# State-space mixer of a streaming encoder: parameters of ten pairs issued ahead of the mixer's inputs, outputs by way of DRAM in large transfers, sines and decays made one stage ahead of their use

## The chip, the cores and the metric

One NeuronCore of one Trainium2 chip runs the whole program in one launch. The metric is device time in microseconds (us), the median of several executions. The kernel before takes 2367.25 us (three runs, 2365.27 to 2368.46). The profile is of one execution of its own.

## The reference

Two layers of an encoder work on 1024 prompt positions and 64 sample positions, 1088 columns in all, of width 1024. Layer 0 mixes by sliding-window attention, layer 1 by a state-space mixer (S5), and each layer ends in a gated convolutional FFN. The change lies in the mixer of layer 1 alone:

```python
xr = jnp.einsum('blgi,gpi->blgp', u_blk, bbr)
xi = jnp.einsum('blgi,gpi->blgp', u_blk, bbi)
...
_, _, sr, si = lax.associative_scan(_affine_combine, (ar, ai, xr, xi), axis=1)
y = jnp.einsum('blgp,gip->blgi', sr, cr) - jnp.einsum('blgp,gip->blgi', si, ci)
...
z = jax.nn.gelu(y).astype(h.dtype)
ag = z @ w_glu + b_glu
out = ag[..., :D_MODEL] * jax.nn.sigmoid(ag[..., D_MODEL:])
```

There are 64 groups of 16 channels, each with a complex state of 64 dimensions that runs along the positions. The final states are outputs too.

## The kernel before, in words

All activations lie with channels on the partitions. Matrix products are done in three passes on split operands (`mm3`, L181 to L183): a high part and a remainder of each operand in a rounded format. So each weight tile of 512 KB is loaded as `raw` (L169, L173), copied to its high part by ScalarE (L175), and its remainder is made by VectorE (L176). `whl` is the pair of both.

**The mixer's stage** (`ssm`) stands between two stretches of dense matmuls: the down projection of the first FFN, and the GLU product of the mixer (`pb`, `pa`). It works on 32 pairs of groups.

- Ahead of it, the normalised input is written to DRAM in a layout by blocks of 8 positions (`hd<-xs`, L873) and read back as four tiles `U` (L917), each of 16 groups, 137 columns (128 prompt blocks, a gap, 8 sample blocks). The row factor is multiplied in afterwards, 8 groups at a time (`ssm_scale`, L923). The factors (`sel`) are ready only when the norm of the last block of columns is.
- The parameters of each pair (522 KB) were worked out during the first FFN and lie in DRAM as `prm`. `params(t)` loads those of two pairs into one tile `pm` of the tag "big", by two DMAs (L952).
- A batch is two pairs (the first two and the last two pairs are batches of one; so there are 18 batches). It goes through stages, with a `yield` between them, and `staged` lets the batches follow each other by one stage. Stage one: ScalarE makes the sines `sc` with both signs (L966) and the decays `rd` (L969); TensorE makes `p1` (L985); VectorE multiplies by cosines (L986) and sines (L990) and adds (L991). Stage two: VectorE runs the scan (L1004) and turns back with two products (L1007, L1008); ScalarE picks the final states into `fin` (L1011). Stage three: TensorE makes `p3` from `U` (L1018, two matmuls a pair) and from the two products (L1023, sixteen a pair); ScalarE copies it into `ys` (L1027). On the page `p1` and `p3` are both called `p`.
- After each fourth pair (a group of 8 channel groups, numbered `kt`, 0 to 7), `ys` is brought into channel order: eight DMAs of 16 partitions each from SBUF to SBUF (`yf<-ys`, L1032). Two stages later ScalarE computes the GELU `z` (L1041, L1043) and its high part `zh` (L1048), and VectorE the remainder `zl` (L1049). These are the operands of the GLU product.

**What sets the order.** Each engine has one in-order queue; a scheduler fixes it when the program is built, from the order in the code and from `self.order(x, first)`, which only forbids x to stand ahead of `first` on an engine. All these loads and stores are issued by SP's queue (SyncE), in order: an entry that has to wait for a semaphore holds all behind it. The order list `turns` puts `sc` and `rd` of a batch behind `fin` of the batch before. The tag "big" has six buffers, shared by `whl`, `pm` and one `U` tile; a `pm` can be loaded once an earlier user of its buffer is done. `sc` and `rd` have two buffers each, PSUM tiles of `p3` six, `p1` two. `U` number 2 lies in "big", number 3 in the buffer of an FFN result (tag "ypB") that has first to be spilled to DRAM (`x<-y`, L1198).

## Time and profile before

| | |
|---|---|
| median of three runs | 2367.25 us (2365.27 to 2368.46) |
| the profiled execution: its own time | 2367.1 us |
| its span (first to last instruction) | 2365.3 us |
| TensorE busy | 2269.7 us, 96% |
| VectorE busy | 1463.6 us, 62% |
| ScalarE busy | 893.6 us, 38% |
| last matmul of the down projection ahead of the mixer | 1197.4 us |
| first matmul of the mixer's pairs | 1222.6 us |
| first matmul of the GLU product | 1354.9 us |

PE is TensorE, DVE is VectorE, ACT is ScalarE, SP is SyncE's queue. "Busy" counts the time in which an instruction of the engine ran. `[7.28 <-X]` behind a row of the timeline says that the engine stood idle for 7.28 us before it, and that X ended that. PEclk is the clock that TensorE was granted, as a share of full speed. A row of the grouped view gives: line, engine, operation, output and inputs, shapes, count; then busy us in total and mean ns of one; then idle us just before them, and what ended it.

### The profile page before, as it was taken

How to read it: one execution, taken by the hardware profiler on the slowest of the kernel's cores; microseconds unless marked ns; L12 is line 12 of the kernel's file. 1: busy time of each engine (PE TensorE's matmuls, PEld its weight loads, DVE VectorE, ACT ScalarE, POOL GpSimd, SP SyncE). 2: the span in 40 equal slices, each digit the busy share in tenths (PEclk: the TensorE clock that was granted, in tenths of full speed). 3: DMA queues.
4: the chain of work that ended last, by engine and by line, in shares of the span. 5: the costliest groups of instructions: out<-in, count | busy, mean ns of one | idle time of the engine just before them, and what ended most of it. 6: DMA issues, size and time to landing. Idle time of an engine off the chain costs nothing. (4 is left out here: it accounts for less than half of the span.)

```text
span 2365.3 us, 35852 instructions
## 1 busy us (share of the span) xinstructions
PE 2269.7 (96%) x14265; PEld 2201.1 (93%) x14265; DVE 1463.6 (62%) x2836; ACT 893.6 (38%) x1463; POOL 282.1 (12%) x286
## 2 busy tenths in 40 slices
PE   8999999999999999999957799999999999999997
PEld 7987799999999999999955699999999999999997
DVE  8677649897577776464557812586555555465554
ACT  5256635322333334444525621343222222154332
POOL 5222006000122311020000100240000000000000
PEclk9999999999999999999967899999999999999998
DMA  5000015322334345664567521242222221165652
GB/s 189 33 30 19 28 50 183 109 69 102 101 130 146 121 137 173 213 213 151 187 209 236 149 70 37 72 157 86 76 82 73 84 73 64 51 211 180 211 176 96
DMA packets 167702, 282.52 MB, mean 119 GB/s; under 512 B 22800, under 2 KB 105264, under 8 KB 167408
## 3 DMA queue, kind: packets, MB, share of 16 engines
q1 hardware_dynamic: 165504, 273.41, 35.9%
q0 software_dynamic: 2032, 6.83, 0.8%
q8 instruction: 112, 1.84, 0.3%
q14 instruction: 54, 0.44, 0.1%
HBM read 210.03 MB, written 65.68 MB: 117 GB/s over the span
## 5 line engine op out<-in xcount | busy, mean ns | idle before, releaser
L181 PE MATMUL mm<-hl,whl 128*128 128x384 f32 (+1 forms) x2232 | 734.9, 330 | 15.5 <-DVE hl L247 8.2
L183 PE MATMUL mm<-hh,whl 128*128 128x384 f32 (+1 forms) x2232 | 733.3, 329 | 1.9 <-DVE whl L176 1.9
L182 PE MATMUL mm<-hh,whl 128*128 128x384 f32 (+1 forms) x2232 | 735.0, 329 | 0.0
L175 ACT ACTIVATE whl<-raw 128x1024 fp32r<-128x1024 f32 x256 | 269.9, 1058 | 707.9 <-PE mm L183 587.9
L176 DVE TENSOR_TENSOR whl<-raw,whl 128x1024 fp32r<-128x1024 f32 x256 | 321.1, 1257 | 224.9 <-ACT whl L175 224.6
L181 PEld LDWEIGHTS mm<-hl,whl 128*128 128x128 f32 x2232 | 420.2, 188 | 17.7 <-DVE hl L247 10.3
L183 PEld LDWEIGHTS mm<-hh,whl 128*128 128x128 f32 x2232 | 420.1, 188 | 2.8 <-DVE whl L176 2.7
L182 PEld LDWEIGHTS mm<-hh,whl 128*128 128x128 f32 x2232 | 420.4, 188 | 0.4
L181 PE MATMUL mm<-gt,whl 128*128 128x384 f32 (+1 forms) x1056 | 346.3, 328 | 2.9 <-ACT y L392 2.3
L182 PE MATMUL mm<-gt,whl 128*128 128x384 f32 (+1 forms) x1056 | 345.5, 327 | 0.0
L183 PE MATMUL mm<-gt,whl 128*128 128x384 f32 (+1 forms) x1056 | 342.6, 327 | 0.7 <-DVE whl L176 0.7
L295 DVE TENSOR_TENSOR u<-rb,mm 128x384 f32<-128x384 f32 (+1 forms) x264 | 132.0, 507 | 285.6 <-PE mm L183 285.4
L181 PEld LDWEIGHTS mm<-gt,whl 128*128 128x128 f32 x1056 | 198.2, 188 | 4.3 <-ACT y L392 2.8
L183 PEld LDWEIGHTS mm<-gt,whl 128*128 128x128 f32 x1056 | 197.9, 188 | 1.0 <-DVE whl L176 1.0
L182 PEld LDWEIGHTS mm<-gt,whl 128*128 128x128 f32 x1056 | 198.3, 188 | 0.0
L303 ACT ACTIVATE t<-u,ppt 128x1090 f32<-128x1090 f32 x88 | 113.5, 1289 | 29.0 <-DVE u L297 15.7
L304 DVE SCALAR_TENSOR_TENSOR t<-u,ppt,t 128x1090 f32<-128x1090 f32 x88 | 119.0, 1352 | 8.6 <-ACT t L303 8.6
L305 DVE SCALAR_TENSOR_TENSOR t<-u,ppt,t 128x1090 f32<-128x1090 f32 x88 | 119.0, 1352 | 1.7
L266 POOL TENSOR_TENSOR y<-y,xl 128x768 f32<-128x768 f32 (+1 forms) x18 | 32.1, 1789 | 622.3 <-DVE y L264 321.7
L318 ACT ACTIVATE t<-t 128x1090 f32<-128x1090 f32 x44 | 49.0, 1114 | 101.0 <-DVE t L305 101.0
L1079 DVE SCALAR_TENSOR_TENSOR y<-pa,ppt,sg 128x384 f32<-128x384 f32 (+1 forms) x24 | 14.2, 594 | 99.6 <-ACT sg L1078 99.6
L1023 PE MATMUL p<-wk,pm 64*128 64x137 f32 x512 | 50.5, 351 | 23.3 <-DVE wk L1007 9.3
(315 smaller groups left out, 3299.0 us busy)
## 6 DMA issues: line engine op xcount, KB each, us to landing
raw<-in_w_down SPq DMA_DIRECT2D x132, 512.0 KB, 4.0
raw<-in_w_up SPq DMA_DIRECT2D x88, 512.0 KB, 3.3
gd<-t SPq DMA_DIRECT2D x44, 512.0 KB, 2.6
pm<-prm SPq DMA_DIRECT2D x32, 522.0 KB, 5.5
gr<-gd SPq DMA_DIRECT2D x28, 384.0 KB, 4.5
xl<-x SPq DMA_DIRECT2D x24, 384.0 KB, 4.0
raw<-in_w_glu SPq DMA_DIRECT2D x16, 512.0 KB, 4.3
gr<-gd SPq DMA_DIRECT2D x22, 320.0 KB, 4.4
```

The costliest lines, as they stand in the source:

```text
L175: nc.scalar.activation(w[:, 0], raw, AF.Copy)
L176: nc.vector.tensor_sub(w[:, 1], raw, w[:, 0].bitcast(F32))
L181: nc.tensor.matmul(out, w[:, 0, sl], xl, start=start, stop=False)
L182: nc.tensor.matmul(out, w[:, 0, sl], xh, start=False, stop=False)
L183: self.last_mm = nc.tensor.matmul(out, w[:, 1, sl], xh, start=False, stop=stop)
L266: by[q].tensor_add(y[:, 2 * q:2 * q + 2], y[:, 2 * q:2 * q + 2], xs[q])
L295: nc.vector.tensor_mul(u[:, t0 + 2:t0 + 2 + np_], rb[:, t0:t0 + np_], ps[:, :np_])
L303: nc.scalar.activation(t, u[:, 0:T + 2], AF.Identity, bias=cb(m), scale=cw(0, m))
L304: nc.vector.scalar_tensor_tensor(t, u[:, 1:T + 3], cw(1, m), t, op0=ALU.mult, op1=ALU.add)
L305: nc.vector.scalar_tensor_tensor(t, u[:, 2:T + 4], cw(2, m), t, op0=ALU.mult, op1=ALU.add)
L318: nc.scalar.activation(ta, ta, AF.Gelu_apprx_tanh)
L1023: nc.tensor.matmul(p3[e], pm[r, i, o:o + P], g_[r, i, c, 0:NC_], start=False, stop=c == 1 and s == 1)
```

## The change

Four things change, all in `ssm` and `ssm_load`.

1. `params` becomes `load`. The `pm` tiles of five steps (ten pairs) are issued at the top of the stage, ahead of the writes and reads of the inputs; then each step t issues tile t+5.
2. `fins[-2]` replaces `turns[0]`: `sc` and `rd` of a batch stand behind `fin` of the batch before the last.
3. `ys` goes to DRAM by one DMA of ScalarE's own queue (`yd<-ys`, L1035) and comes back as `yf` by one DMA of SP (`yf<-yd`, L1040), one stage later, behind a `pm` load. The GELU follows three stages behind instead of two, and behind the last `yd` write issued.
4. `U` number 2 and number 3 change places ("ypB" and "big"), the spill moves ahead of `U` 2, `U` 3 is loaded from step 6 on, and the first two weight tiles of the GLU stand behind the last `pm`.

```diff
-        if q == 2:
+        if q == 3:
             u = self.big([P, 16, NC_], "U", F32)
         else:
-            u = self.yp.tile([P, 16, NC_], F32, name="U", tag="ypB" if q == 3 else "ypA", bufs=1 if q == 3 else 2)
+            u = self.yp.tile([P, 16, NC_], F32, name="U", tag="ypB" if q == 2 else "ypA", bufs=1 if q == 2 else 2)
...
+        yd = self.dram.tile([D, 8, NC_], F32, name="yd")
...
+            tiles, got, fins, out = {}, {}, [self.last_rs] * 2, [None]
+
+            def load(t):
+
+                pm = self.big([P, 2, PRM], "pm", F32)
+                for e in range(2):
+                    got[t] = nc.sync.dma_start(pm[:, e], self.prm[:, 2 * t + e])
+                tiles[t] = [pm]
+            for t in range(5):
+                load(t)
+            self.order(self.hw[0], got[4])
             us = [self.ssm_load(0)]
...
                 if e0 == 0:
-                    params(t)
+                    if t + 5 < 16:
+                        load(t + 5)
...
                 for c in range(2):
                     x = nc.scalar.activation(sc[:, :, c], pm[:, :, OSI:PRM], AF.Copy, scale=(1.0, -1.0)[c])
-                    self.order(x, turns[0])
+                    self.order(x, fins[-2])
                 for e, q in enumerate(qs):
                     x = nc.scalar.activation(rd[:, e], mask[:, None, :].to_broadcast([P, 2, 138]), AF.Copy, scale=self.rho[:, q:q + 1])
-                    self.order(x, turns[0])
+                    self.order(x, fins[-2])
                 if qs[-1] == 31:
                     self.wsrc.pop(0)
-                    self.load_ahead(AHEAD)
+                    for j in range(AHEAD):
+                        self.load_ahead(1 + j)
+                        self.order(self.loaded, got[15])
...
                 if qs[0] == 2:
+                    self.order(self.spill(), self.last_u)
                     us.append(self.ssm_load(2))
-                if qs[0] == 4:
-                    self.order(self.spill(), self.last_u)
+                if qs[0] == 12:
                     us.append(self.ssm_load(3))
...
-                turns[0] = x
+                fins.append(x)
...
+                    out.append(nc.scalar.dma_start(yd[kt * P:kt * P + P].rearrange("(g i) t c -> (i t) g c", i=16), ys[0]))
                     yf = self.t4([P, 8, NC_], "yf")
-                    for g_ in range(8):
-                        x = nc.sync.dma_start(yf[16 * g_:16 * g_ + 16], ys[0][:, g_])
-                        if g_ == 0:
-                            yx.append((kt, x))
+
                     if kt < 7:
-
+                        yield
+                    x = nc.sync.dma_start(yf, yd[kt * P:kt * P + P])
+                    if t + 6 in got:
+                        self.order(x, got[t + 6])
+                    if kt < 7:
                         yield
                         yield
...
                     self.order(x, out[0])
+                    self.order(x, out[-1])
```

**SP's queue at the start of the mixer's stage**, as a difference (+ is the changed kernel, - the kernel before; `hd` and `U` are the inputs on their way through DRAM, `pm` the parameters):

```order
-L952 DMA pm<-prm 128x1044 x4
+L937 DMA pm<-prm 128x1044 x12
 L873 DMA hd<-xs 128x1096 x2
 L917 DMA U<-hd 128x8x137
+L873 DMA hd<-xs 128x2x1096 x2
+L917 DMA U<-hd 128x8x137
 L873 DMA hd<-xs 128x2x1096
-L917 DMA U<-hd 128x8x137
-L873 DMA hd<-xs 128x2x1096 x2
-L917 DMA U<-hd 128x8x137 x4
-L952 DMA pm<-prm 128x1044 x2
-L1198 DMA x_91<-y 1024x1x320
```

Twelve parameter loads (six tiles; the sixth is that of step 0's `load(5)`) instead of four stand ahead of the first write of the inputs, and the second half of `U` 0 stands behind two more writes.

**ScalarE's queue in the middle of the stage.** Before, `wk_11998` holds pairs 14 and 15, and `sc_12071` and `rd_12072` belong to pairs 16 and 17:

```order
L1011 COPY fin_11455<-wk_11998 128x8 x2
L966 ACTIVATE sc_12071<-pm_12068 128x2x138 x2
L969 ACTIVATE rd_12072<-mask_11456,rho_276 128x276 x2
L1027 ACTIVATE ys_12107<-p3_12095 128x137
L1027 ACTIVATE ys_12107<-p3_12096 128x137
L1027 ACTIVATE ys_12107<-p3_12110 128x137
L1027 ACTIVATE ys_12107<-p3_12111 128x137
L1041 ACTIVATE z_12157<-yf_12054 128x1024
```

In the changed kernel `wk_11925` holds pairs 12 and 13, `sc_12053` and `rd_12054` belong to pairs 16 and 17 again, and `z_12077` is the GELU of `kt` 2:

```order
L1016 COPY fin_11471<-wk_11925 128x8 x2
L969 ACTIVATE sc_12053<-pm_11710 128x2x138 x2
L972 ACTIVATE rd_12054<-mask_11472,rho_276 128x276 x2
L1032 ACTIVATE ys_11965<-p3_12015 128x137
L1032 ACTIVATE ys_11965<-p3_12016 128x137
L1016 COPY fin_11471<-wk_11996 128x8
L1032 ACTIVATE ys_11965<-p3_12029 128x137
L1032 ACTIVATE ys_11965<-p3_12030 128x137
L1035 DMA yd_11442<-ys_11965 128x8x137
L1016 COPY fin_11471<-wk_11996 128x8
L1048 ACTIVATE z_12077<-yf_11910 128x1024
```

The sines of pairs 16 and 17 stand one `fin` earlier, and a DMA issue stands among ScalarE's instructions, ahead of the GELU of the group before.

**VectorE's queue at the end of the stage**, from the last product of the last batch of two on. Before:

```order
L1008 TENSOR_TENSOR wk<-wk,sc 128x552
L990 TENSOR_TENSOR wk<-sc,p_12497 128x2x137
L991 TENSOR_TENSOR wk<-wk 128x2x137
L1004 SCALAR_TENSOR_TENSOR wk<-rd,wk 128x276
L1007 TENSOR_TENSOR wk<-wk,pm 128x276
L1008 TENSOR_TENSOR wk<-wk,sc 128x276
L990 TENSOR_TENSOR wk<-sc,p_12555 128x2x137
L991 TENSOR_TENSOR wk<-wk 128x2x137
L1004 SCALAR_TENSOR_TENSOR wk<-rd,wk 128x276
L1007 TENSOR_TENSOR wk<-wk,pm 128x276
L1008 TENSOR_TENSOR wk<-wk,sc 128x276
```

In the changed kernel:

```order
L1013 TENSOR_TENSOR wk<-wk,sc 128x552
L176 TENSOR_TENSOR whl<-raw,whl 128x1024
L996 TENSOR_TENSOR wk<-wk 128x2x137
L991 TENSOR_TENSOR wk<-pm,p_12514 128x2x137
L1058 TENSOR_TENSOR zl<-z,zh 128x384 x2
L1058 TENSOR_TENSOR zl<-z,zh 128x320
L1009 SCALAR_TENSOR_TENSOR wk<-rd,wk 128x276
L995 TENSOR_TENSOR wk<-sc,p_12514 128x2x137
L1012 TENSOR_TENSOR wk<-wk,pm 128x276
L996 TENSOR_TENSOR wk<-wk 128x2x137
L1013 TENSOR_TENSOR wk<-wk,sc 128x276
L1009 SCALAR_TENSOR_TENSOR wk<-rd,wk 128x276
```

The two single pairs run side by side, and remainders of weights and of `z` that stood elsewhere stand between their steps. Before the last product of the stage VectorE has made four weight remainders (L176) in the kernel before and five in the changed one; of the sets of `zl`, six in both. On TensorE's queue, nine matmuls of the GLU stand ahead of the last group of `p3` matmuls before; in the changed kernel 23 stand ahead of the last six of them.

More of the change, by code (lines that the diff above doesn't have):

```diff
@@ L945, in ssm @@
             ROWS = (slice(0, 64), slice(64, 128))
-            tiles, got, turns, out = {}, {}, [self.last_rs], [None]
-            def params(t):
-                pm = self.big([P, 2, PRM], "pm", F32)
-                for e in range(2):
-                    got[t] = nc.sync.dma_start(pm[:, e], self.prm[:, 2 * t + e])
-                sc = self.wts.tile([P, D], F32, name="sc", tag="raw", bufs=2) if t < 8 else self.yp.tile([P, D], F32, name="sc", tag="ypA", bufs=2)
-                sc = sc[:, :552].rearrange("p (e c k) -> p e c k", e=2, c=2)
-                rd = sp.tile([P, 2, 2, 138], F32, name="rd", bufs=2)
-                tiles[t] = pm, sc, rd
             def batch(qs):
@@ L961, in batch @@
                 if e0 == 0:
-                    params(t)
+                    if t + 5 < 16:
+                        load(t + 5)
+                    sc = self.wts.tile([P, D], F32, name="sc", tag="raw", bufs=2) if t < 8 else self.yp.tile([P, D], F32, name="sc", tag="ypA", bufs=2)
+                    tiles[t] += [sc[:, :552].rearrange("p (e c k) -> p e c k", e=2, c=2), sp.tile([P, 2, 2, 138], F32, name="rd", bufs=2)]
                 pm, sc, rd = tiles[t]
@@ L1042, in batch @@
                     self.order(x, out[0])
+                    self.order(x, out[-1])
                     x = nc.scalar.activation(z[:, SEQ:].rearrange("p (c t) -> p c t", t=8), yv[:, 129:137], AF.Gelu_apprx_tanh)
                     self.order(x, out[0])
+                    self.order(x, out[-1])
                     for b, (t0, n_) in enumerate(BLK):
@@ L1049, in batch @@
                         nc.vector.tensor_sub(zl[b][:, kt], z[:, t0:t0 + n_], zh[b][:, kt].bitcast(F32))
-            yx, scans = [], []
+            scans = []
             self.staged([batch(x) for x in [[0], [1]] + [[q, q + 1] for q in range(2, 30, 2)] + [[30], [31]]], oldest=True)
-            for kt, x in yx:
-                if kt < 5:
-                    self.order(x, got[2 * kt + 6])
             fo = sp.tile([P, P], F32, name="fo")
```

## The prediction

> **What bounds the kernel now.** The page comes first, for the span, and then the windows over the mixer's stage, fifty microseconds a row.
>
> ```profile
> span 2365.3 us, 35852 instructions
> 1200.00:1250.00 50.00, 27.14 (x188) 22.16 (x189) 32.00 (x63) 16.64 (x48) 5.08 (x16) 0.59 0.81 268
> 1250.00:1300.00 50.00, 33.41 (x310) 28.05 (x310) 34.02 (x57) 25.89 (x73) 2.15 (x12) 0.76 0.74 220
> 1300.00:1350.00 50.00, 35.20 (x376) 29.67 (x373) 42.92 (x69) 30.42 (x86) 6.46 (x15) 0.91 0.55 163
> 1350.00:1400.00 50.00, 50.00 (x317) 48.98 (x316) 15.52 (x26) 18.74 (x37) 0.55 (x1) 0.96 0.26 79
> ```
>
> The columns are the stretch, its length, busy PE, weight loads, DVE, ACT and POOL, then the granted clock, the DMA share and GB/s. From 1350 on TensorE is full, and the GLU product and the second FFN behind it are the same instructions in both kernels. So the time that the mixer's stage saves or loses ahead of its first GLU matmul moves the end of the kernel by as much. In the three rows before that no engine is full; VectorE is the busiest in the second and third. The grouped view of 1222 to 1355 us says what it does and what it waits for.
>
> ```profile
> L1023 PE MATMUL p<-wk,pm 64*128 64x137 f32 x496 | 49.3, 353 | 23.3 <-DVE wk L1007 9.3 <-DVE wk L1008 8.0 <-issue 3.3
> L1018 PE MATMUL p<-U,pm 128*128 128x137 f32 x128 | 25.7, 345 | 7.7 <-ACT ys L1027 7.7
> L985 PE MATMUL p<-U,pm 128*64 128x137 f32 x256 | 23.3, 324 | 6.8 <-DMA pm<-prm 2.4 <-issue 2.3 <-PE p L1023 0.9
> L1004 DVE TENSOR_TENSOR_SCAN wk<-rd,wk 128x552 f32<-128x552 f32 (+1 forms) x18 | 21.2, 1179 | 1.4
> L986 DVE TENSOR_TENSOR wk<-pm,p 128x274 f32<-128x274 f32 x32 | 13.2, 433 | 4.1 <-DMA hd<-xs 2.2 <-PE p L985 1.5 <-issue 0.5
> L990 DVE TENSOR_TENSOR wk<-sc,p 128x274 f32<-128x274 f32 x32 | 13.0, 436 | 11.8 <-ACT sc L966 11.8
> L991 DVE TENSOR_TENSOR wk<-wk 128x548 f32<-128x548 f32 (+1 forms) x18 | 12.0, 666 | 1.8
> L1007 DVE TENSOR_TENSOR wk<-wk,pm 128x552 f32<-128x552 f32 (+1 forms) x17 | 11.5, 679 | 0.3
> L1008 DVE TENSOR_TENSOR wk<-wk,sc 128x552 f32<-128x552 f32 (+1 forms) x17 | 11.5, 678 | 0.3
> L923 DVE TENSOR_TENSOR U<-U,sel 128x1096 f32<-128x1096 f32 (+2 forms) x9 | 10.3, 1155 | 1.7 <-ACT sel L907 1.7
> L1049 DVE TENSOR_TENSOR zl<-z,zh 128x384 fp32r<-128x384 f32 (+1 forms) x18 | 9.0, 529 | 12.3 <-ACT zh L1048 12.3
> L176 DVE TENSOR_TENSOR whl<-raw,whl 128x1024 fp32r<-128x1024 f32 x4 | 4.9, 1219 | 0.0
> ```
>
> VectorE's rows sum to 21.2 + 13.2 + 13.0 + 12.0 + 11.5 + 11.5 + 10.3 + 9.0 + 4.9 = 106.6 us of work in 133 us. The idle column sums to 33.7 us, more than the 26.4 left over, because neighbouring instructions overlap a little. Of that idle time 24.1 us stand in two rows, and both name ScalarE: 11.8 us for the sines, 12.3 us for `zh`. Yet ScalarE worked only 16.64 + 25.89 + 30.42 = 73 us of 150 in the windows: it is late, not busy. Its timeline shows why.
>
> ```profile
> 1264.59 1.28 ACT L1041 ACT_TABLE_LOAD   x1 [7.28 <-DMA pm<-prm]
> 1265.89 2.03 ACT L1041 ACTIVATE z<-yf 128x1024 f32<-128x1024 f32 x1
> 1268.45 0.89 ACT L1048 ACTIVATE zh<-z 128x384 fp32r<-128x384 f32 x2
> ...
> 1269.01 0.56 DVE L1049 TENSOR_TENSOR zl<-z,zh 128x384 fp32r<-128x384 f32 x1 [7.92 <-ACT zh L1048]
> 1281.23 0.79 DVE L990 TENSOR_TENSOR wk<-sc,p 128x274 f32<-128x274 f32 x2 [4.16 <-ACT sc L966]
> ...
> ACT z L1041 <- DMA yf<-ys: 6.2, 2, 3.4
> ```
>
> The first GELU stands at the head of ScalarE's queue and waits 7.3 us for a transfer. The releaser is given as `pm<-prm`, but `z` reads only `yf`, whose eight issues stand in SP's queue between `pm` loads (1032 between 952); behind it wait `ys`, `fin` and the sines, and VectorE loses 7.92 us before its first `zl`; the second GELU costs it 4.16 us at the sines in the same way. The other wait recurs in every batch; here is one, from VectorE's timeline and ScalarE's.
>
> ```profile
> 1301.96 0.73 DVE L1008 TENSOR_TENSOR wk<-wk,sc 128x552 f32<-128x552 f32 x1
> 1303.61 0.79 DVE L990 TENSOR_TENSOR wk<-sc,p 128x274 f32<-128x274 f32 x2 [0.93 <-ACT sc L966]
> 1302.72 0.20 ACT L1011 COPY fin<-wk 128x8 f32<-128x8 f32 x1 [1.14 <-DVE wk L1008]
> 1302.83 0.75 ACT L966 ACTIVATE sc<-pm 128x276 f32<-128x276 f32 x2
> ```
>
> VectorE ends L1008, ScalarE copies the final states, only then makes the next sines, and VectorE stands still for 0.93 us.
>
> **The sines and decays.** With `fins[-2]` the sines of a batch stand behind the `fin` of a batch that VectorE left a whole batch ago, about 82.4 us (the first six VectorE groups) over 16 batches' worth of pairs = 5.15 us earlier. Two buffers each suffice: the one that is needed was last read by the batch before the last. So the 0.93 us wait goes, and with it nearly all of the 11.8 us; I leave 1 us for the first batches. **Gain 10.8 us** (bounds 7, if the 4.16 us that the second GELU causes there come back, and 11.8).
>
> **The outputs through DRAM.** Eight issues become one write by ScalarE and one read by SP, and the GELU moves back by one batch. These rows bound the trip (KB each, median us from issue to landing).
>
> ```profile
> pm<-prm SPq DMA_DIRECT2D x32, 522.0 KB, 5.5
> U<-hd SPq DMA_DIRECT2D x8, 548.0 KB, 8.6
> yf<-ys SPq DMA_DIRECT2D x64, 68.5 KB, 3.2
> hd<-xs SPq DMA_DIRECT2D x2, 548.0 KB, 3.2
> ```
>
> The write has the size of a `hd` write (3.2 us), the read that of a `pm` load (5.5): 8.7 us, or 17.2 if both were like the `U` reads, which ran while the DMA was full. From `kt` 3 on the read is ordered behind a `pm` load that needs `p3` of the next batch, so one batch more: 106.6 / 16 = 6.7 us + 5.5 = 12.2. The GELU stands behind the next group's `yd`, two batches or 13.3 us later. So it is covered by 1 to 4 us, and the 7.92 of the 12.3 us that VectorE lost at the first GELU goes; the other 4.4 us, in three places, are `zl` standing close behind `zh`, and I leave them. **Gain 7.9 us** (bounds: nothing, to 12.3).
>
> On ScalarE the write's issue is new. An issue on SP took this long:
>
> ```profile
> L917 SPq DMA_DIRECT2D U<-hd x8: 359/924/4535, 1214.0 to 1245.8; - x8
> ```
>
> That is 0.36 to 4.5 us, median 0.9. Eight times 0.9 us are 7 us more on an engine that idles half the time; with the read's thin cover I put **1.5 us lost** for both (bounds 0 and 16; the upper end is the second rival).
>
> The Trainium skill, "Perfetto Trace Analysis", section "DMA Instruction — HWDGE", says that the issuing sequencer is held from the moment its semaphores are met, first for the lock of a descriptor generator used by one issuer at a time, then until the descriptors are made. The spread from 0.36 to 4.5 us agrees with such a lock; no run here shows an issue on ScalarE yet. By that rule with the long end each time the sum would lose 36 us of ScalarE time instead of 7, and the gain above would be gone.
>
> **The parameters ahead.** TensorE waited for `pm` only 2.4 us in all (row L985), so little is gained by having them early; I count nothing, and the bound is 2.4 us. What they may delay are the inputs:
>
> ```profile
> 1194.21 1.76 SPq L952 DMA_DIRECT2D pm<-prm  x4
> 1211.25 0.80 SPq L873 DMA_DIRECT2D hd<-xs  x2
> 1214.03 0.37 SPq L917 DMA_DIRECT2D U<-hd  x1
> 1195.00:1205.00 10.00, 4.94 (x28) 4.22 (x26) 3.45 (x10) 1.00 (x2) 0.00 (x0) 0.78 0.57 214
> 1222.08 1.37 DVE L923 TENSOR_TENSOR U<-U,sel 128x274 f32<-128x274 f32 x2 [1.66 <-ACT sel L907]
> ```
>
> Four loads moved at 214 GB/s for a share of 0.57, which is 375 GB/s when full. Twelve loads of 522 KB are 6.4 MB or 17.1 us; begun at 1194.2 they drain at 1211.3 at the earliest, and a few us later with a start that the row does not show; the first `hd` write is issued at 1211.25. `U` may be some 2 us later, but VectorE took it up at 1222.08 only when `sel` came. **0.5 us lost** (bounds 0 and 2). The swap of `U` 2 and 3, the earlier spill and the later `w_glu` loads cost nothing: `U` 2 is first used after the scan of pairs 10 and 11, and SP held up by the spill has only loads behind it whose buffers are not free yet.
>
> **The end of the stage.**
>
> ```profile
> 1354.88 0.44 PE L181 MATMUL pb<-zl,whl 128*128 128x384 f32 x1
> 1356.66 1.21 PE L1023 MATMUL p<-wk,pm 64*128 64x137 f32 x16
> ```
>
> Nine GLU matmuls fit between these two rows, 1.78 us or 0.2 us each. The changed order has 23 ahead of the last `p3` instead of 9, in gaps where TensorE waits for VectorE: **gain 2.4 us**. VectorE has one weight remainder more before its last product (1219 ns): **1.1 us lost**, as it overlaps.
>
> **TensorE as the next bound.** Its three groups took 49.3 + 25.7 + 23.3 = 98.3 us, 6.1 us for a batch, against VectorE's 6.7. VectorE, no longer held up, will now and then wait for `p1`. How much, the trace of before does not show. The bounds: nothing at the clocks of before (mean of the three windows 0.75), since 98.3 is below 106.6; and 18 us if the clock of the first window, 0.59, held throughout (98.3 x 0.75 / 0.59 = 125 against 106.6). I take **2.5 us lost**, near the low end, since VectorE waited for `p1` only 1.5 us (row L986).
>
> The Trainium skill, "TensorE: Matmul & The Clock Gate", section "Part 1: The HAM clock gate", knows only a half and a full clock and gives the full one after a few us of sustained work; the granted 0.59, 0.76 and 0.91 above would be mixtures. By that rule a denser stage runs more at the full clock, TensorE's share shrinks, and the 2.5 us would be near nothing.
>
> **The sum.** 10.8 + 7.9 + 2.4 - 1.5 - 0.5 - 1.1 - 2.5 = 15.5 us gained. The profiled execution took 2367.1 us, 1.8 over its span and 0.15 below the median; so 2367.1 - 15.5 = 2351.6.
>
> **The rivals.** First, *TensorE or ScalarE's queue takes over half of what is freed*: the order of `z`, `yd`, `ys` and `fin` in one queue makes new waits of about a microsecond a batch. For it: 98.3 against 106.6 us, and the thin cover of 1 to 4 us. Against it: VectorE hardly waits for TensorE today. The lower ends of the two main terms, 7 us of the sines and nothing of the `z` wait, give 2367.1 - 7 = 2360 us. Chance 0.2.
>
> Second, the other side, *ScalarE held by its own DMA issues*: place, L1035, once per `kt`; price, up to 4.5 us each and a read that then lands behind the GELU's turn. A `kt` has 13.3 us, of which ScalarE works some 73 / 150 x 13.3 = 6.5; issue and trip cost something once together they exceed 13.3 us, and they eat the whole gain of 20 us once they exceed it by 2.5. With both ends as the `U` reads, 17.2 us and 4.5 for the issue, each of eight groups stalls 8.4 us, 67 us in all, less the 20 gained: 2414. At half of that, 4.2 us a group, 34 - 20, it is 2381. Against it: the DMA share falls from 0.81 to 0.55 along the stage. Chance 0.05.
>
> Third, *all of VectorE's waits go*: 4.4 us at `zl` and the 2.4 at `pm` as well, nothing lost to TensorE: 2351.6 - 4.4 - 2.4 - 2.5 = 2342. Chance 0.08. Fourth, *the change does little*: the early loads are no gain, and the waits for sines turn into equal ones for `zh` or `p1`: 2365. Chance 0.05.
>
> **How the numbers follow.** The forecast, 2351.6, has the remaining 0.62. The range runs from 2344, short of the third case, to 2361, past the first: what it leaves out is the slow case, the fourth and most of the third, about 0.18. A measurement of this kernel tells about 0.2%, 4.7 us, from no change. Faster by more: forecast, first and third, 0.90. Same: the fourth, 0.05. Slower: 0.05.
>
> **What would show it.** Right: no idle row of L995 before ScalarE's sines beyond 2 us in all; no wait of the first GELU over 2 us; the first GLU matmul near 1338 and TensorE full from there. Wrong: `yd` issues of several us on ScalarE; `z` waiting for `yf` in most groups; L991 waiting for `p1` by more than 5 us; VectorE below 85% busy between the first and the last scan.

## The result, and the profile after

| | before | after |
|---|---|---|
| first measurement, median | 2366.82 us (4 runs, 2365.27 to 2368.46) | 2348.43 us (4 runs, 2343.79 to 2350.72) |
| the same two kernels measured again (e9) | 2365.85 us (9 runs) | 2342.89 us (4 runs, 2339.30 to 2344.70) |
| the profiled execution: own time, span | 2367.1, 2365.3 us | 2347.37, 2345.6 us |
| VectorE's first scale to its last product | 1222.08 to 1355.51 us | 1223.99 to 1339.93 us |
| first GLU matmul | 1354.88 us | 1332.30 us |
| last sigmoid of the GLU | 1550.56 us | 1531.68 us |

The ratio is 0.992 with an interval of 0.9903 to 0.9937, and 0.9903 (0.9889 to 0.9916) in the second measurement. The change makes the kernel 18 to 23 us faster; 15.5 were forecast.

The windows over the stage after the change come first; the last row takes VectorE's whole share of the stage (columns as above).

```profile
1200.00:1250.00 50.00, 24.43 (x193) 20.35 (x193) 34.61 (x68) 19.64 (x56) 5.37 (x17) 0.69 0.94 335
1250.00:1300.00 50.00, 43.74 (x430) 35.79 (x432) 45.23 (x74) 31.05 (x92) 2.19 (x15) 0.87 0.76 239
1300.00:1350.00 50.00, 43.15 (x376) 36.94 (x373) 37.45 (x62) 31.45 (x80) 2.37 (x11) 0.93 0.74 214
...
1224.00:1341.00 117.00, 97.61 (x919) 80.61 (x921) 101.40 (x169) 68.53 (x203) 5.37 (x33) 0.86 0.79 245
```

The same stretch of the kernel before:

```profile
1222.00:1356.00 134.00, 96.59 (x886) 80.73 (x887) 101.81 (x167) 69.08 (x201) 9.67 (x33) 0.79 0.72 220
```

VectorE does the same work, 101.4 us instead of 101.8, in 117 us instead of 134. Its idle time falls from 32.2 to 15.6 us. The granted clock rises from 0.79 to 0.86. Where the idle time went is in the grouped view of VectorE, 1222 to 1345 us, after the change:

```profile
L1009 DVE TENSOR_TENSOR_SCAN wk<-rd,wk 128x552 f32<-128x552 f32 (+1 forms) x18 | 21.1, 1176 | 0.9
L991 DVE TENSOR_TENSOR wk<-pm,p 128x274 f32<-128x274 f32 x32 | 13.9, 433 | 5.4 <-PE p L990 4.9 <-issue 0.5
L995 DVE TENSOR_TENSOR wk<-sc,p 128x274 f32<-128x274 f32 x32 | 13.7, 431 | 0.6 <-ACT sc L969 0.6
L996 DVE TENSOR_TENSOR wk<-wk 128x548 f32<-128x548 f32 (+1 forms) x18 | 11.9, 664 | 1.2
L1013 DVE TENSOR_TENSOR wk<-wk,sc 128x552 f32<-128x552 f32 (+1 forms) x18 | 11.9, 665 | 0.3
L1012 DVE TENSOR_TENSOR wk<-wk,pm 128x552 f32<-128x552 f32 (+1 forms) x18 | 11.9, 664 | 0.3
L923 DVE TENSOR_TENSOR U<-U,sel 128x1096 f32<-128x1096 f32 (+2 forms) x9 | 10.3, 1154 | 1.7 <-ACT sel L907 1.7
L1058 DVE TENSOR_TENSOR zl<-z,zh 128x384 fp32r<-128x384 f32 (+1 forms) x21 | 10.1, 530 | 4.4 <-ACT zh L1057 4.4
L176 DVE TENSOR_TENSOR whl<-raw,whl 128x1024 fp32r<-128x1024 f32 x5 | 6.1, 1216 | 4.9 <-ACT whl L175 4.9
```

The wait for sines is 0.6 us (11.8 before), that for `zh` 4.4 (12.3), of which 2.7 stand behind the last product. New are 4.9 us before the weight remainders; the wait for `p1` has grown from 1.5 to 4.9. The timelines of ScalarE and VectorE show the first GELU, then one batch, then the two new waits at weight remainders:

```profile
1260.65 0.37 ACTq L1035 DMA_DIRECT2D yd<-ys  x1
1261.05 1.28 ACT L1048 ACT_TABLE_LOAD   x1 [0.43 <-ACT ys L1032]
1262.35 2.05 ACT L1048 ACTIVATE z<-yf 128x1024 f32<-128x1024 f32 x1
...
1307.25 0.75 ACT L969 ACTIVATE sc<-pm 128x276 f32<-128x276 f32 x2
1311.48 0.73 DVE L1013 TENSOR_TENSOR wk<-wk,sc 128x552 f32<-128x552 f32 x1
1312.08 0.37 ACTq L1035 DMA_DIRECT2D yd<-ys  x1
1312.48 0.43 DVE L995 TENSOR_TENSOR wk<-sc,p 128x274 f32<-128x274 f32 x1
1315.77 2.05 ACT L1048 ACTIVATE z<-yf 128x1024 f32<-128x1024 f32 x1 [3.08 <-DMA yf<-yd]
1316.66 0.73 DVE L1013 TENSOR_TENSOR wk<-wk,sc 128x552 f32<-128x552 f32 x1
1319.38 1.06 ACT L175 ACTIVATE whl<-raw 128x1024 fp32r<-128x1024 f32 x1
1320.48 1.22 DVE L176 TENSOR_TENSOR whl<-raw,whl 128x1024 fp32r<-128x1024 f32 x1 [3.08 <-ACT whl L175]
...
1337.69 1.06 ACT L175 ACTIVATE whl<-raw 128x1024 fp32r<-128x1024 f32 x1 [3.28 <-DMA raw<-in_w_glu]
1338.79 1.22 DVE L176 TENSOR_TENSOR whl<-raw,whl 128x1024 fp32r<-128x1024 f32 x1 [1.79 <-ACT whl L175]
```

The first GELU no longer waits for a transfer. The sines made at 1307.25 are used at 1312.48, and VectorE goes from L1013 by way of L991 (1312.13) to L995 without idle time. At 1315.77 the fifth GELU waits 3.08 us for its `yf`; the weight's high part stands behind it on ScalarE, and VectorE, with the remainder at the head of its queue, loses the same 3.08 us. The second wait has another cause: at 1337.69 ScalarE stands 3.28 us until a weight tile of the GLU has landed (`raw<-in_w_glu`), and VectorE loses 1.79 us before the last product of the stage.

The DMA issues between 1190 and 1352 us, with KB each and the median time to landing:

```profile
pm<-prm SPq DMA_DIRECT2D x32, 522.0 KB, 7.1
U<-hd SPq DMA_DIRECT2D x8, 548.0 KB, 6.7
yd<-ys ACTq DMA_DIRECT2D x8, 548.0 KB, 8.0
yf<-yd SPq DMA_DIRECT2D x8, 548.0 KB, 3.7
```

And the view of the line of the write alone:

```profile
L1035 ACTq DMA_DIRECT2D yd<-ys x8: 366/366/383, 1249.2 to 1344.8; - x8
DMA to landing us min/median/max: 5.9/8.0/12.0
```

The write took 8.0 us and the read 3.7, almost the reverse of the 3.2 and 5.5 that the prediction took from similar rows; the sum, 11.7, is inside its bounds. Every read is issued within 0.1 us of the landing of its write, so it is the write alone that made the trip long: in the two groups whose GELU waited it took 12.0 and 11.1 us, in stretches where the DMA share was 0.88 and 1.03 (a transfer counts where it starts), against 0.79 in the stage as a whole. The issue costs ScalarE 0.37 us each time.

TensorE's groups up to 1339 us, and below them its timeline at the end of the stage:

```profile
L1028 PE MATMUL p<-wk,pm 64*128 64x137 f32 x500 | 46.6, 327 | 8.1 <-issue 4.1 <-DVE wk L1012 3.3 <-DVE wk L1013 0.7
L1023 PE MATMUL p<-U,pm 128*128 128x137 f32 x128 | 27.5, 346 | 6.9 <-ACT ys L1032 6.9
L990 PE MATMUL p<-U,pm 128*64 128x137 f32 x256 | 22.8, 318 | 3.4 <-issue 2.5 <-PE pr L902 0.9
```

```profile
1332.30 0.43 PE L181 MATMUL pb<-zl,whl 128*128 128x384 f32 x1
...
1340.42 0.97 PE L1028 MATMUL p<-wk,pm 64*128 64x137 f32 x12 [1.35 <-DVE wk L1013]
```

TensorE's idle time in the three groups falls from 37.8 to 18.4 us. Between these last two rows it runs GLU matmuls and two shorter groups of `p3`: 26 GLU matmuls stand ahead of the last `p3`, against 9 before.

### The profile page after: what moved, and what is told of

The parts are those of the page before. It is cut to its first block, busy times and chain, and to the rows that moved or that the text cites. A ratio compares the mean times of both kernels' runs of the same rounds, so it can differ in the third digit from the quotient of the medians.

```text
span 2345.6 us, 35751 instructions
## 1 busy us (share of the span) xinstructions
PE 2267.0 (97%) x14265; PEld 2197.5 (94%) x14265; DVE 1460.2 (62%) x2836; ACT 893.7 (38%) x1463; POOL 277.5 (12%) x286
## 5 line engine op out<-in xcount | busy, mean ns | idle before, releaser
L176 DVE TENSOR_TENSOR whl<-raw,whl 128x1024 fp32r<-128x1024 f32 x256 | 320.7, 1255 | 232.5 <-ACT whl L175 229.7
L1085 DVE SCALAR_TENSOR_TENSOR y<-pa,ppt,sg 128x384 f32<-128x384 f32 (+1 forms) x24 | 14.1, 592 | 95.5 <-ACT sg L1084 95.5
L370 DVE TENSOR_TENSOR gt<-gr,gt 128x768 fp32r<-128x768 f32 (+2 forms) x70 | 57.9, 864 | 17.5 <-ACT gt L369 17.5
```

The costliest lines, as they stand in the source:

```text
L176: nc.vector.tensor_sub(w[:, 1], raw, w[:, 0].bitcast(F32))
L370: nc.vector.tensor_sub(x[:, 1, j:j + e], raw, x[:, 0, j:j + e].bitcast(F32))
```

## The experiments

Two lengths read from each trace go with the times. V is from VectorE's first scale to the start of its last product, T from there to the last sigmoid of the GLU. A term worth something on VectorE shows in V, one at TensorE's end in T. The starts of the stage differ between executions by up to 5 us (1219.21 to 1224.09), and so does what follows the last sigmoid (812.7 to 817.6 us, the same code in all); V and T leave both out. "GLU" counts the GLU matmuls ahead of the last `p3`, "weights" the weight remainders (L176, 1.2 us each) that stand inside V. The scheduler orders each variant anew, so both counts move with edits that are not about them. The fourth item of the change (the places of `U`, the spill, the later GLU weights) stands in all variants of the changed kernel; no run takes it out by itself.

| kernel | median us | ratio to before (95%) | V | T | GLU | weights |
|---|---|---|---|---|---|---|
| before | 2365 to 2367 | | 133.4 | 195.1 | 9 | 4 |
| after | 2348.43 | 0.992 (0.9903 to 0.9937) | 115.9 | 191.8 | 26 | 5 |
| e1 sines late | 2358.53 | 0.9976 (0.9967 to 0.9985) | 122.5 | 198.2 | 0 | 3 |
| e2 outputs old | 2352.50 | 0.9948 (0.9936 to 0.9961) | 117.3 | 199.0 | 1 | 3 |
| e3 parameters late | 2342.38 | 0.9908 (0.9892 to 0.9923) | 113.6 | 192.6 | 26 | 5 |
| e4 write on SP | 2345.83 | 0.9921 (0.9908 to 0.9935) | 112.8 | 195.3 | 9 | 3 |
| e5 sines only | 2353.31 | 0.9952 (0.994 to 0.9965) | 119.3 | 195.6 | 15 | 4 |
| e6 outputs only | 2359.18 | 0.9974 (0.9964 to 0.9983) | 125.1 | 196.1 | 9 | 4 |
| e7 cover less | 2354.76 | 0.9962 (0.9948 to 0.9975) | 122.1 | 196.6 | 15 | 3 |
| e8 cover more | 2345.32 | 0.9916 (0.9902 to 0.9929) | 109.2 | 196.7 | 1 | 3 |
| e9 after again | 2342.89 | 0.9903 (0.9889 to 0.9916) | 114.5 | 192.0 | 26 | 5 |
| e10 halves | 2339.77 | 0.9892 (0.9879 to 0.9906) | 110.0 | 191.4 | 26 | 5 |
| e11 late, more cover | 2345.54 | 0.9925 (0.9911 to 0.9938) | 112.1 | 196.8 | 1 | 3 |
| e12 as e11, halves | 2345.58 | 0.9917 (0.9903 to 0.9931) | 111.8 | 196.8 | 0 | 3 |

Three groups shared a chip and its runs of the kernel before: e1 to e4, e5 to e8, e9 to e12.

What makes T is in the windows from the last product to the last sigmoid, here of the kernel before and of the changed one:

```profile
1355.51:1550.56 195.05, 194.84 (x1195) 194.31 (x1195) 67.32 (x122) 53.52 (x83) 15.59 (x10) 1.00 0.21 66
1339.93:1531.68 191.75, 190.76 (x1167) 189.91 (x1168) 66.14 (x122) 54.12 (x80) 15.60 (x10) 1.00 0.23 72
```

TensorE is busy for all of T but 0.2 and 1.0 us, and for 98.9% or more of it in every run. So T is the TensorE work that is left when the last product begins: 1149 of the GLU's 1152 matmuls before, 1126 after, 1126 to 1130 in the four executions with 26 ahead, 1143 to 1152 in the other ten. The 15 of e5 and e7 bring little, since 28 `p3` matmuls and 1148 of the GLU are still left there. In e1 and e2 alone the granted clock within T was below 1.00 (0.99 and 0.98), and their T is 1.3 to 2.3 us longer than that of e8, e11 and e12, with as many GLU matmuls left.

**e1: the sines put back.**

```diff
-                    self.order(x, fins[-2])
+                    self.order(x, fins[-1])
```

> The changed kernel with its sines and decays put back behind the `fin` of the batch just ahead (`fins[-1]` for `fins[-2]`). My theory, by the sum's term of 10.8 us with bounds 7 to 11.8: about 10 us slower than the changed kernel, 2357 to 2361 us, and VectorE's second product (L995) waits for `sc` by 9 to 12 us in all again, some 0.9 us a batch. Rival, the waits only change names: VectorE would wait for `zh`, `p1` or the weights instead, and the time stays within 3 us of the changed kernel, 2346 to 2352.

2358.53 us, 10 us above the first and 16 above the second measurement of the changed kernel. VectorE's groups in e1, 1222 to 1345 us:

```profile
L995 DVE TENSOR_TENSOR wk<-sc,p 128x274 f32<-128x274 f32 x32 | 13.1, 437 | 10.3 <-ACT sc L969 10.0
```

The wait is back at 10.0 us, as my theory has it; the waits had not merely changed names. But V grows by only 6.6 us, and T by 6.4: no GLU matmul stands ahead of the last `p3` here, and two remainders fewer inside V. The profiled execution is also the slowest of ten, 2363.75 us. So this run mixes the wait with the order at the end; e5 separates them.

**e2: the outputs as before.** The write and the read give way to the eight transfers of the kernel before.

```diff
-                    out.append(nc.scalar.dma_start(yd[kt * P:kt * P + P].rearrange("(g i) t c -> (i t) g c", i=16), ys[0]))
...
-                    x = nc.sync.dma_start(yf, yd[kt * P:kt * P + P])
+                    for g_ in range(8):
+                        x = nc.sync.dma_start(yf[16 * g_:16 * g_ + 16], ys[0][:, g_])
```

> The changed kernel with its outputs moved as before: eight transfers a `kt` from `ys` to `yf`, issued by SP, the GELU two stages behind; the early parameters and early sines stay. My theory, by the sum's term for the outputs (7.9 gained, 1.5 lost): 5 to 9 us slower than the changed kernel, 2354 to 2358, and the `zh` wait of `zl` back at 8 us or more. Rival, it was the early parameters that freed the first GELU (SP's queue no longer holds `pm` loads among the `yf` issues): within 2 us of the changed kernel, and the first GELU waits 1 us or less here too. A second rival, the new trip through DRAM costs more than it frees (its landings were 8.0 and 3.7 us): 2 to 5 us faster than the changed kernel.

2352.50 us: 4 to 10 us slower than the changed kernel, a little under the numbers I gave. VectorE's groups in e2, 1222 to 1345 us, and below them the first GELU:

```profile
L1052 DVE TENSOR_TENSOR zl<-z,zh 128x384 fp32r<-128x384 f32 (+1 forms) x21 | 10.4, 530 | 11.5 <-ACT zh L1051 11.5
...
1254.02 1.28 ACT L1044 ACT_TABLE_LOAD   x1 [2.10 <-DMA pm<-prm]
1257.98 0.56 DVE L1052 TENSOR_TENSOR zl<-z,zh 128x384 fp32r<-128x384 f32 x1 [7.43 <-ACT zh L1051]
```

The wait for `zh` is back at 11.5 us though the parameters are early. Yet it is not quite the wait of the kernel before: the first GELU waits 2.10 us here instead of 7.28, and VectorE still loses 7.43 before its first `zl` (7.92). VectorE came to that `zl` at 1250.55, when ScalarE had sines, decays, `ys`, the table load and the GELU itself still to do. So early parameters take most of the first GELU's wait for its transfer, and the loss at `zl` stays while the GELU stands only two stages behind. The rival that has the new trip costing more than it frees falls too.

**e3: the parameters loaded at their own batch.**

```diff
-            for t in range(5):
-                load(t)
-            self.order(self.hw[0], got[4])
...
-                    if t + 5 < 16:
-                        load(t + 5)
+                    load(t)
```

> The changed kernel with each pair's parameters loaded at the batch that uses them, none ahead of the inputs; early sines and the trip through DRAM stay. My theory, which counted the early parameters at nothing (bound 2.4 us): 0 to 3 us slower than the changed kernel, 2347 to 2352. Rival, the early loads are what lets the rest work, since a read of `yf` on SP and the loads of `pm` otherwise hold each other up: 8 us slower or more, 2356 and up, with the first GELU waiting several us for `yf` and TensorE for `pm`.

2342.38 us, faster than my theory's range and far from the rival's. Against e9's 2342.89 it is no difference. V and T are within 2.4 and 0.8 us of the changed kernel's. The early parameters are worth nothing that these runs can tell, and if they cost anything it is under the spread. The edit does one thing more: `got[t + 6]` is not there yet when it is asked for, so the read of `yf` no longer stands behind a `pm` load either. In this run neither ScalarE nor TensorE has a wait for `pm`, though each `pm` is loaded at its own batch as in the kernel before.

**e4: the write issued by SP.**

```diff
-                    out.append(nc.scalar.dma_start(yd[kt * P:kt * P + P].rearrange("(g i) t c -> (i t) g c", i=16), ys[0]))
+                    out.append(nc.sync.dma_start(yd[kt * P:kt * P + P].rearrange("(g i) t c -> (i t) g c", i=16), ys[0]))
```

> The changed kernel with the write of `yd` issued by SP instead of ScalarE. My theory: ScalarE pays 0.37 us for each of eight issues, little of it on the path, so taking them away gains at most 1.5 us; SP now waits for `ys` and for the write with its loads behind both, which costs 0 to 4 us: 2347 to 2353. Rival, ScalarE is held by its own issues (or the write's landing of 8.0 us is long because of the queue it is on, where SP's reads land in 3.7): 3 us faster or more, 2345 and below, with the write landing in 4 us or less.

2345.83 us, between the two measurements of the changed kernel. The line of the write in e4:

```profile
L1035 SPq DMA_DIRECT2D yd<-ys x8: 370/374/427, 1246.0 to 1339.0; - x8
DMA to landing us min/median/max: 4.4/6.3/9.5
```

Taking the issues off ScalarE gains nothing that these runs can tell, and the write still lands in 6.3 us, not in the 4 that the rival asks for. With 0.37 to 0.38 us an issue in the changed kernel, ScalarE is not held by its own issues. The Trainium skill, "DMA: Bandwidth & Descriptors", section "Issuing engines are not separate DMA queues", says that transfers end up on the same DMA engines whoever starts them, so that another issuer saves issue time only. This pair of runs agrees: 0.37 us an issue either way, and the changed kernel's own median landing was 8.0 us in one execution and 6.8 in e9.

**e5: the sines alone, in the kernel before.**

```diff
-            tiles, got, turns, out = {}, {}, [self.last_rs], [None]
+            tiles, got, turns, out = {}, {}, [self.last_rs] * 2, [None]
...
-                    self.order(x, turns[0])
+                    self.order(x, turns[-2])
...
-                turns[0] = x
+                turns.append(x)
```

> The kernel before with nothing but the sines and decays one stage ahead. Putting them back cost the changed kernel 10 to 13 us; alone, with the first and second GELU still stuck behind late transfers, my theory gives less: the 7 us of the sum's lower bound up to 10, so 2355 to 2358 us by a kernel before of 2365. Rival, the two halves are independent and add up: 13 us, 2352. Second rival, the sines gain only where the outputs come in time: 0 to 3 us, 2362 to 2365.

2353.31 us, 11.8 below the kernel before; V falls by 14.1 us and T stays. That is nearer to the additive rival than to my 7 to 10. Its VectorE groups, 1222 to 1355 us:

```profile
L990 DVE TENSOR_TENSOR wk<-sc,p 128x274 f32<-128x274 f32 x32 | 13.8, 433 | 5.6 <-ACT sc L966 5.6
...
L1049 DVE TENSOR_TENSOR zl<-z,zh 128x384 fp32r<-128x384 f32 (+1 forms) x21 | 10.4, 529 | 8.1 <-ACT zh L1048 8.1
```

Stuck GELUs do keep sines late, as I argued, but they account for 3.4 of the 5.6 us (two waits, 0.72 and 2.71); another 1.6 stand before sines that wait for their own `pm`. And the wait for `zh` fell as well, from 12.3 to 8.1, which I had not counted on. My expectation of a loss between the halves falls.

**e6: the outputs alone.** The changed kernel with the edits of e1 and e3 together.

> The changed kernel with its sines put back and its parameters loaded at their own batch: of the change, the trip through DRAM, the order of the `U` loads and the later weight loads are left. My theory: the outputs' 6 to 8 us remain, 2357 to 2360 us by a kernel before of 2365, and `zl` waits for `zh` by 4 us or less. Rival, without early parameters the GELU stalls as in the kernel before, because the late `pm` loads hold the read of `yf` up: 0 to 3 us below the kernel before, 2362 to 2365.

2359.18 us, 6.0 below the kernel before and inside my range; V falls by 8.4 us. Its VectorE groups, 1222 to 1355 us:

```profile
L991 DVE TENSOR_TENSOR wk<-sc,p 128x274 f32<-128x274 f32 x32 | 13.1, 437 | 9.6 <-ACT sc L965 9.4
...
L1054 DVE TENSOR_TENSOR zl<-z,zh 128x384 fp32r<-128x384 f32 (+1 forms) x21 | 10.3, 529 | 3.5 <-ACT zh L1053 3.5
```

The wait for `zh` goes (3.5 us are left), that for sines stays, without any early parameters. Alone, the two parts gave 11.8 and 6.0, together 17.8; the whole change gave 18 to 23.

**e7: the GELU one batch earlier.**

```diff
                     if kt < 7:
                         yield
-                        yield
                     z = self.t4([P, T], "z")
```

> The changed kernel with the GELU one batch earlier, so that the trip through DRAM has some 6.7 us of cover instead of 13.3. The trip as the changed kernel's profile has it is 8.0 us for the write and 3.7 for the read, 11.7 in the median. My theory, cover decides: each of seven groups waits some 5 us at `z`, 35 us of ScalarE's time of which its idle half absorbs part, so 10 to 25 us slower than the changed kernel, 2357 to 2372, with `z` waiting for `yf` in most groups. Rival, ScalarE has time enough for that and VectorE goes on meanwhile: within 4 us, 2345 to 2351.

2354.76 us, 6 to 12 us slower than the changed kernel. Groups of ScalarE and VectorE in e7, 1222 to 1355 us:

```profile
L1047 ACT ACTIVATE z<-yf 128x1024 f32<-128x1024 f32 x7 | 14.5, 2074 | 12.7 <-DMA yf<-yd 12.7
...
L1057 DVE TENSOR_TENSOR zl<-z,zh 128x384 fp32r<-128x384 f32 (+1 forms) x21 | 10.5, 529 | 16.5 <-ACT zh L1056 16.5
```

`z` now waits in six of seven groups and VectorE loses 16.5 us before `zl`, more than before the change. So the place of the GELU decides, though not by the transfer alone: before the first `zl` VectorE loses 6.87 us and `z` waits only 1.53 of them, as in e2 with its old transfers. V grows by 6.1 us over the changed kernel; T grows by 4.9 with the order at the end. What no run has is the eight transfers of the kernel before with the GELU three stages behind. So how much of the outputs' gain is the trip through DRAM, and how much the later GELU, stays open. The size was off, 12.7 us of waits at `z` and not 35: the trip took 6.0 + 3.8 us in the median here instead of 11.7, and a GELU's turn came 5.8 to 11.6 us behind its write (from the `yd` issue to `z`, less its wait), not 6.7.

**e8: one batch more of cover** for the first six groups.

```diff
                         yield
                         yield
+                    if kt < 6:
+                        yield
                     z = self.t4([P, T], "z")
```

> The changed kernel with the GELU of the first six groups one batch later still, some 20 us of cover. The changed kernel's `z` waited 4.2 us for `yf` in all, and 4.9 us at the weights' remainders hang on the second of those waits. My theory: that cover is what is short in two groups, so 2 to 5 us faster, 2342 to 2346, with no wait of `z` over 0.5 us before the last two groups. Rival, the later GELU only moves work towards the end of the stage, where the last groups and the weights stand together: the same or up to 4 us slower, 2347 to 2351.

2345.32 us: within my range, but between the two measurements of the changed kernel, so no gain can be told. On ScalarE the mechanism shows: of the first seven GELUs only the first waits, 0.91 us, and not for `yf`. It waits for the landing of the second group's write: `ys`, `yf` and `z` share five buffers (tag "t4"), and its `z` gets the one that this write reads. V falls by 6.7 us, 3.8 of it work that has left it (two weight remainders, 2.4, and a set of `zl`, 1.4). Of the 4.9 us at the remainders that I had hung on the fifth GELU, 3.08 were its own; the 1.79 are those of the late GLU weight. Yet from the first scale to the last sigmoid only 1.7 us are gained, because T grows by 5.0. The timelines of VectorE and TensorE in e8 at the end of the stage:

```profile
1331.02 0.45 DVE L1013 TENSOR_TENSOR wk<-wk,sc 128x276 f32<-128x276 f32 x1
1331.82 0.44 PE L181 MATMUL pb<-zl,whl 128*128 128x384 f32 x1
1332.19 0.97 PE L1028 MATMUL p<-wk,pm 64*128 64x137 f32 x12
```

One GLU matmul instead of 26 stands ahead of the last `p3`. Twenty-five of 0.2 us are 5.0 us: what VectorE gained was given back on TensorE. My theory saw only the first half of that; the rival's late work at the stage's end is nearer, though it named other work.

**e9: the changed kernel again.**

> The changed kernel itself, unchanged, beside the three that follow, since several of the differences told from it (parameters late, write on SP, more cover) are as small as its own spread of 2344 to 2351 us. All theories: the ratio of 0.992 again, 2345 to 2349 us by a kernel before of 2365.

2342.89 us, 2 us under the range: two measurements of one kernel differ by 5.5 us in the median, by 0.0017 in the ratio, with overlapping intervals. Differences between variants of less than some 5 us from different groups are therefore not told here.

**e10: the write in two halves**, the first after two of a group's four pairs.

```diff
+                if qs[-1] % 4 in (1, 3):
+                    kt, h = qs[-1] // 4, qs[-1] % 4 // 2
+                    r = kt * P + 64 * h
+                    out.append(nc.scalar.dma_start(yd[r:r + 64].rearrange("(g i) t c -> (i t) g c", i=16), ys[0][:, 4 * h:4 * h + 4]))
                 if qs[-1] % 4 == 3:
-                    kt = qs[-1] // 4
-                    out.append(nc.scalar.dma_start(yd[kt * P:kt * P + P].rearrange("(g i) t c -> (i t) g c", i=16), ys[0]))
```

> The changed kernel with the write of `yd` in two halves, the first one issued after two of the four pairs, so that only 32 rows of 16 partitions' worth are left for the second. My theory: the second half lands in 4 to 6 us instead of 8, the two waits of `z` for `yf` (4.2 us) go, and 1 to 4 us are gained over the changed kernel; eight issues more on ScalarE cost 8 x 0.37 us of its idle time. Rival, a landing is mostly a fixed cost or queueing: the second half takes 7 us or more as well, and the time is within 1 us or up to 3 us slower.

2339.77 us, the fastest of all: 3.1 below e9 in the median. The intervals of the two ratios overlap, so the gain is likely and not certain. The line of the write in e10:

```profile
L1036 ACTq DMA_DIRECT2D yd<-ys x16: 366/366/379, 1242.5 to 1337.3; - x16
DMA to landing us min/median/max: 3.1/4.6/9.9
```

A half lands in 4.6 us, and none of the first seven GELUs waits for a transfer; V falls by 4.5 us against e9, and with 26 GLU matmuls in the same place T keeps it. The Trainium skill, "DMA: Bandwidth & Descriptors", section "Rules for kernel authors", says that two transfers to disjoint partition halves are not worth making, since both share the same DMA engines. The case here is another one: each half takes all 128 partitions of `ys` and half of its channel groups, and the first leaves two pairs earlier.

**e11 and e12: combinations.** e11 has the edits of e3 and e8, e12 those of e10 as well.

> The changed kernel with parameters loaded at their own batch and the GELU of the first six groups one batch later. If the early parameters cost some 2 us (the single change gave 2342.4 beside 2345 to 2348) and the cover is worth 1 to 2 us, both together give 3 to 5 us over the changed kernel, 2341 to 2344. Rival, both differences were the spread of the measurement, and TensorE decides the end: within 1 us of the changed kernel in the same job.

> The version before this one with the write of `yd` in two halves as well. With 20 us of cover the trip through DRAM is hidden for all groups but the last, so the halves gain nothing ahead of it; the last group's trip is hidden by the GLU products of the seven other groups. My theory: within 1 us of the version without halves. Rival, the last group's trip holds the end of the stage: 2 us faster or more.

2345.54 and 2345.58 us. In e11 the two small differences did not add, and my theory falls: it is 2.6 us slower than e9, which is outside the rival's 1 us too. Both kernels have V near 112 us and T at 196.8, with one GLU matmul or none ahead of the last `p3`. The wait for a buffer that e8 had is longer here: the first GELU of e11 stands 2.82 us and that of e12 3.27 us until the second group's write has landed, and VectorE loses 4.92 and 4.78 us before its first `zl`. With 20 us of cover the halves gain nothing, as I said for e12, but the trip is not all hidden: the extra batch runs into the five buffers. No run gives "t4" a sixth.

## Why the prediction was right, point by point

The direction, the range of 2344 to 2361 us and the two main mechanisms held. The second measurement, 2342.89, lies a little under the range's lower end. The prediction's own signs came out so: L995 idle 0.6 us in all (at most 2 wanted), the first GELU waits 0.43 us and not for a transfer (at most 2). The first GLU matmul came at 1332.30, ahead of the 1338 that were named, and TensorE was not full from there: up to the last product it worked 6.8 of 7.6 us, on GLU and `p3` matmuls in turn. Of the signs against it, `yd` issues took 0.38 us at most, `z` waited for `yf` in two of the first seven groups (the eighth waited 9.4 us, beside a full TensorE), and VectorE was busy 90% between its first and last scan (91.7 of 101.8 us). L991 waited 4.9 us for `p1`, just under the 5 that I had named, and 5.5 in e9.

- **Sines and decays, 10.8 us.** In the changed kernel's rows 11.8 fell to 0.6, a gain of 11.2. Alone (e5) they gave 11.8 us in the time.
- **Outputs through DRAM, 7.9 us.** Of 12.3 us before `zl`, 4.4 were to stay, and 4.4 did; but 2.7 of them stand behind the last product, where they do not hold the scans up. Ahead of it the gain is 12.3 - 1.7 = 10.6. Alone (e6) the outputs gave 6.0 us with their own costs, against 7.9 - 1.5 = 6.4 in the sum. The trip was not the one that was priced: the write took 8.0 us instead of 3.2, the read 3.7 instead of 5.5, and no read was held behind a `pm` load, for which the prediction added a batch of 6.7 us. That the sums lie close, 11.7 and 12.2, is luck. And the trip is only part of the edit: with the GELU two stages behind, VectorE waits 11.5 us for `zh` with the old transfers (e2) and 16.5 with the new ones (e7), so the third stage is needed for the gain; that the trip is needed too is not shown.
- **Issue and cover, 1.5 us lost, and the weight remainder, 1.1.** 4.9 us stand before the weight remainders. Of them 3.08 are the late `yf` at 1315.77, twice the 1.5 that were set aside. The other 1.79 stand before the fifth remainder, whose weight landed late; the prediction had counted the later GLU weight loads at nothing. Whether their later place is the cause, no run tells by itself. The remainder's own work, 1.1, does not show in the sum, for VectorE's busy time inside V fell from 101.4 to 100.7 us. The thin cover was real, at two of the first seven groups (e8 and e10 remove those waits), but the loss shows at L176, not at `zl`. The issues themselves cost nothing that e4 could find. The Trainium skill's rule of a lock on the descriptor generator ("Perfetto Trace Analysis", section "DMA Instruction — HWDGE") has the issuing sequencer wait for its turn. With the longest issue of the trace before, the prediction made that 36 us of ScalarE's time. None of it is seen: with eight issues or sixteen, none on ScalarE took over 0.40 us.
- **Parameters ahead, nothing, and 0.5 us lost at the inputs.** e3 finds nothing in the time either way.
- **TensorE as the next bound, 2.5 us lost.** The wait for `p1` grew by 3.4 us, but L991's idle time as a whole only from 4.15 to 5.37, since the earlier wait for `hd` in that row is gone: 1.2 lost. The granted clock rose with the denser stage, 0.79 to 0.86, but the mean of L1028 fell only from 353 to 327 ns and that of L1023 not at all (345, 346). By the Trainium skill's rule on the clock gate ("TensorE: Matmul & The Clock Gate", "Part 1: The HAM clock gate"), a half clock that turns full after some us of sustained work, the loss would be near nothing, as the prediction read it. The 1.2 us lost lie about half way between that and its 2.5.
- **GLU matmuls ahead of the last `p3`, 2.4 us.** T is 3.3 us shorter: 23 matmuls of the GLU and four of `p3` fewer are left at the last product, TensorE has 4.1 us less to do and stands still 0.8 us more. The prediction's own figures, 14 matmuls of 0.2 us, give 2.8 and not 2.4. This term rests on the order alone, and it decides more than I thought. The four executions with 26 ahead have T between 191.4 and 192.6 us, the other ten between 195.1 and 199.0. That what is left makes T shows in TensorE's busy time; what brings the 26 about does not. The same four have five weight remainders inside V, the others three or four, and no experiment moved either count by itself.

The trace adds up: V is 17.5 us shorter, T 3.3, together 20.8. The stage began 1.9 us later and what follows the GLU took 0.8 us less: 20.8 - 1.9 + 0.8 = 19.7, which is the difference of the two profiled executions. Set against the sum, the 20.8 us are 11.2 for the sines (10.8 forecast), 10.6 for the outputs (7.9) and 3.3 for the end of TensorE (2.4), less 4.9 at the weight remainders (1.5) and 1.2 at L991 (2.5). VectorE's other small idle times gave 1.1 more and its busy time 0.7, where 1.1 were to be lost to the remainder; the 0.5 for the inputs did not show. So the forecast of 15.5 came near partly because errors of both signs stand in it: the outputs 2.7 too low, the waits at the remainders 3.4 too low.

Of the rivals, the first (2360 us, half lost to queues) did not come about: the new waits are 4.9 us at the weights and 1.2 at L991, together under a third of what was freed. The second, ScalarE held by its own issues, is refuted by the issue rows (0.38 us at most) and by e4. Its other half, a trip that is longer than its cover, came about in two groups, 4.2 us in all, and in e7 in six. The prediction held against it that the DMA share falls along the stage, to 0.55; in the changed kernel it ends at 0.74. The third gave 2342 us, close to e9, but not by its mechanism, since waits for `zh`, `p1` and the weights remain. The fourth falls with e5 and e6.

## What to carry to other kernels

When a busy engine stands idle before an instruction whose maker is itself mostly idle, look at what stands ahead of the maker in its queue: moving the making one stage earlier was worth 11.8 us here, alone, and cost no buffer. Price a transfer by its cover, from issue to the turn of its reader: the reader one batch earlier cost 6 to 12 us here, order at the end included, and sending half of the data as soon as it exists shortened V about as much as a batch more of cover (110.0 and 109.2 us) and did not run into the shared buffers. And where a scheduler orders the end of a stage, read the order again after each edit: some 25 matmuls that moved behind the last wait (e8) took back 5.0 of the 6.7 us that were won ahead of it.

## What the runs showed of the hardware

In the nine executions with eight whole writes, a write of 548 KB to DRAM in pieces of 548 bytes landed in 5.7 to 8.2 us in the median, and a read of the same bytes in rows of 4384 bytes in 3.6 to 4.3. Half the write landed in 4.6 (e10) and 5.2 (e12). An issue of such a write on ScalarE's queue took 0.37 us in the median and 0.40 at most, beside some 60 issues of SP in the same 160 us.

The granted clock of the same stage moved with how closely it was packed: within V it was 0.79 before (133.4 us), 0.86 after (115.9) and 0.90 in e10 (110.0). The mean time of the matmuls followed only in part: with the clock 9% higher (0.79 to 0.86), L1028 took 7% less and L1023 the same.
